# Attention scores of layer 1: the lo parts of q over all 128 rows beside zeros, the cached keys in a gap of the bias tile

## The chip, the cores and the metric

The kernel runs on one core of a Trainium2 chip. The metric is device time in microseconds (us), lower is better. A core has a tensor engine (PE; its weight loads are listed apart, as PEld), a vector engine (DVE), a scalar engine (ACT), GpSimd (POOL) and a sync engine (SP) whose queue issues nearly all DMAs here. Each engine works through its own list of instructions in order and waits for others by semaphores.

## What is computed

Two layers of a transformer trunk for 128 prompt tokens and 256 sample tokens, all in float32, D = 1024. Layer 0 has two recurrent mixers, layer 1 attention with 16 heads of 64 channels; an MLP ends each layer. Only layer 1's attention and the projection after it are touched by the change. In the reference, cut to that:

```python
qp, kp, vp = _na_qkv(hp, w_qkv_na[o], qn_na[o], kn_na[o])         # prompt: q and k with RMS norms per head
mp = _merge(_ctx_attention(qp, kp, vp)) @ w_out_na[o]              # softmax(q k / 8) v over the prompt's 128 keys
qs, ks_, vs = _na_qkv(hs, w_qkv_na[o], qn_na[o], kn_na[o])
ms = _merge(_na_latent(qs, ks_, vs, cache_na_k[:, o], cache_na_v[:, o], rpb_na[o])) @ w_out_na[o]
...
xp = xp + p_g1 * mp                                                # gates per condition: prompt, sample
xs = xs + s_g1 * ms
```

`_na_latent` puts a window of own keys (with a relative bias) and 128 cached keys into one softmax.

## The kernel before

**Products in parts.** Products of float32 accuracy are made of three products of rounded parts: hi times hi, lo times hi and hi times lo. ACT makes the hi part of a weight block (L211), DVE the lo part (L212). The main products have 128 rows of weights and 128 columns.

**Layer 1.** `layer1` runs over four groups b of 4 heads. For each it makes q, k (`attn_qk`) and v (`attn_v`) with the products of `tm_half` (L689 to L691, 256 columns each), loads the bias of the 4 heads (`na_bias`: 12 DMAs from DRAM into a tile of tag `bz`, L1532), and between these parts takes steps of the attention of the group before (`attn_heads`, `attn_pair`). After the loop come the steps of the last group, beside the first products of the output projection (`proj_residual`; its products are L674 to L676).

**q and k of a pair of heads** are transposed on PE (L1592; the cached keys L1604) to features by tokens, two heads in the 128 rows. For q the hi part is scaled out of PSUM by ACT (L1598), the lo part by one DVE instruction over 128 x 384 (L1599) into the tile `ql`. DMAs (L1588) copy the parts: `qd[:, e]` holds head e's hi part twice, in either half of the rows; `ks[:, e]` holds head e's hi part of k in its own half of the rows and the lo part in the other half.

**The scores of a head** are three pieces (prompt, two halves of the sample) of 256, 384 and 384 columns. Each is two products into the same PSUM piece: L1642 takes `qd` over 128 rows (hi of q with both parts of k), L1643 takes `ql` and `ks` over the 64 rows of the head alone (lo of q with hi of k). So a head has six products, by turns with 128 and 64 rows. DVE adds the bias and takes the maximum (L1649), ACT the exponentials (L1654), DVE the division (L1657), PE the transposes (L1662, L1666), ACT and DVE their copies (L1663, L1667), PE the products with v, by turns in the two column halves of the array (L1677, form 128*64).

```python
nc.tensor.matmul(p, qd[:, e, kt % 2, tt], ks[:, e, kt % 2, c], start=True, stop=False)
nc.tensor.matmul(p, ql[r, kt % 2, tt], ks[r, e, kt % 2, c], start=False, stop=True)
```

**Memory.** Tiles are taken from slots by tag, in turn (`sb`): a tile waits until the one that had its slot is done with. In layer 1's pool the tag `m4` has two slots. `attn_tiles` puts all cached keys (`kc`, one DMA, L1567) and all cached values (`vc`, L1569) in them; in the rows of the trace both are named `m`. After the attention `spread_gate` (called by `proj_residual`) takes two more tiles of this tag, the gates of prompt and sample spread over the partitions: `m<-gs`, L515, 512 KB each.

**After the attention** `residual` multiplies the projection's sums by the gate (L1273, per token tile and column half: prompt tile 0 reads the first gate tile, sample tiles 1 and 2 the second) and adds them to x (L1275, the first column half on POOL), and `norm` runs by token tile: squares on ACT (L544), L546, POOL's power (L528), the scaling of one half on DVE (L549) and the other on ACT (L550), transposes on PE (L555), then shift, scale and parts (L560 to L567). The MLP's first products (L1340 to L1342) need the tiles 0 and 1.

**Order.** The order of each engine is set by a scheduler at build time, from the order of the code, the slots and its own estimate of durations; `behind` pins a few places.

Of the kernel before, what the change touches and what calls it, by code (L numbers as in the profile page):

```python
# [30 lines left out]
# the levels inside blocks of 32  # L31
NS = 5
# the MLP's first blocks take the last token tile later, so that they need not wait for its norm
BEHIND = 2
# order of issue: what is put behind which marked instructions (see Trunk.behind) on their engines.
# "split", "group": weights and products (by column tile) of the first parts (PARTS); "gate1", "gate2": products of the output
# gates, by half of the rows; "proj", column half, token tile, half of the rows; "last": the last products of the MLPs,
# by layer, token tile and column half; T: a norm's transposes, by token tile and half; D, A: its last steps on VectorE
# and ScalarE (rD, rA: of the first norm); sel: of the modulation; s, out: of DeltaNet's states and outputs
# [11 lines left out]
# the first norm's features (row tiles) in parts, of which the modulation and the first products are taken one by one  # L51
PARTS = [range(0, 2), range(2, 4), range(4, 6), range(6, 8)]
# order of the mixers' part: h, d: steps of HGRN2 and DeltaNet (n of them), a: of the modulation; 256 columns of products:
# f: forget gates (2 direction + half), q: HGRN2's q, c: q, k, v of DeltaNet (of 6), v: values, g: output gates;
# m: output of HGRN2
# [4 lines left out]
# steps of the modulation beside the blocks of the two MLPs  # L60
PUMP = [0, 0, 4, 4] + [3, 4] * 6, [0] * 6 + [1] * 9 + [0]
# block of an MLP at which its gate is read
GATE_AT = 15
# halves of blocks of weights (of w1 by number, of the mixers' as in STEPS) whose lo part GpSimd takes, and the level at
# which it takes the products of HGRN2's gates
# [4 lines left out]
# names of the 128 x 128 constant matrices, in their order in the constants' array  # L70
# [3 lines left out]
def make_consts():  # L74
    """Constants that depend on shapes alone: matrices [128, n, 128] (row index a, column index b); per level L the
    pairs of positions in different halves of one block of 2L (levels up to 16 only inside the 32 x 32 blocks on the
    diagonal, [128, 32], behind the identity), side by side; and [128, 64] the column windows."""
# [11 lines left out]
    # column windows of the neighbourhood attention; queries (rows, twice 64) in reversed column order  # L89
# [7 lines left out]
class Halves:  # L97
    """[128, 8, n] as two tiles [128, 4, n], indexed as one."""
# [9 lines left out]
class Trunk:  # L108
# [15 lines left out]
    def open(self, name, **bufs):  # L124
        """A pool for a part of the program; bufs: slots by tag. Pools close in the reverse order."""
        st = self.ctx.enter_context(ExitStack())
        self.pools.append((st, bufs, st.enter_context(self.tc.tile_pool(name=name, bufs=1))))
# [4 lines left out]
    def banks(self, **tags):  # L132
        """PSUM's banks by tag, taken in turn, for a part of the program."""
        self.bank = {tag: list(b) for tag, b in tags.items()}
# [8 lines left out]
    def behind(self, *key):  # L143
        """What is traced here is issued behind the instructions that ORDER names, on their engines."""
# [34 lines left out]
    def split_tiles(self, tag):  # L179
        """Tiles of the hi and lo parts of [128, 8, 384]."""  # L180
        tiles = [self.sb([P, 4, T], tag, F32R) for _ in range(4)]
        return Halves(tiles[0::2]), Halves(tiles[1::2])
# [4 lines left out]
    def mixc(self, shape, name, dt=F32):  # L187
        """A tile that lasts as long as layer 0's mixers."""
# [12 lines left out]
    def slab(self, src, a, b, ring=""):  # L201
        """[128, a, b] of a weight matrix, in two halves along a."""
# [11 lines left out]
    def split_w(self, raws, a, b, ring="", pool=()):  # L214
        """hi and lo parts of a slab: functions of the index along a. pool: the halves whose lo part GpSimd takes."""
# [11 lines left out]
    def start(self):  # L227
# [47 lines left out]
        # silu(cond) by row tile, [128, 2 kt + cond]; a column tile takes 32 columns, of which the first two count  # L275
        self.sc = self.const([P, 2 * KT + 30], "scz")
        nc.gpsimd.memset(self.sc, 0.0)
        # column (kind, cond): 1 in rows 64 g + 32 kind + cond
# [6 lines left out]
    def params_ada(self):  # L285
        """The modulation's bias and the norms' gains, feature-major."""
# [5 lines left out]
    def params(self):  # L292
# [6 lines left out]
        # lower bound of the forget gate: softmax over the 3 rows, the first row of its running sum  # L299
# [16 lines left out]
    def ada_quad(self, l, cols, take):  # L316
        """Four blocks of 512 columns (from cols) of silu(cond) @ ada_w, one per column tile of the array:
        take(rows, psum [128, 512]), of block j the two conditions in rows 32 j and 32 j + 1. In steps."""
# [15 lines left out]
    def ada_sums(self, l, col, take):  # L334
        """1024 columns (from col) of silu(cond) @ ada_w, with the products on the other engines, beside the MLP's on
        the tensor engine, which takes only the sums over the partitions: take(psum [128, 512]), of half n of the
        columns condition v in row 64 v + 32 n. In steps."""
# [18 lines left out]
    def ada_half(self, l, col, take):  # L356
        """1024 columns (from col) of silu(cond) @ ada_w: column tile 2 g + n of the array takes half g of the rows and
# [1415 lines left out]
```

## Time and profile before

| | |
|---|---|
| time, median of 3 runs | 1180.23 us (1179.6 to 1186.71) |
| span of the profiled execution | 1183.9 us |
| its own time | not listed apart; of the three runs only the one of 1186.71 us is longer than this span |
| PE busy | 1127.1 us, 95% |
| DVE, ACT, POOL busy | 65%, 42%, 24% |
| share of the chain that ended last | PE 79%, POOL 6%, DVE 6%, DMA 6% |
| layer 1's attention | about 726 to 883 us of the span |

A matmul's record has a start and a modelled end; ends overlap the next starts. The pace is read from start to start. "128*128" is the part of the array that a product uses (rows by columns); 64*128 is half of its rows. Idle time is listed with what released it.

### The profile page before, as it was taken

The page shows a single profiled execution, that of the slowest core. Times are in us where ns is not written, and L with a number is a line of the kernel's source. Part 1 is how long each engine was busy: PE and PEld are TensorE (multiplying, and loading weights), DVE is VectorE, ACT ScalarE, POOL GpSimd, SP SyncE. Part 2 cuts the span into 40 slices and gives each one's busy share as a digit, 9 for nine tenths or more (in the row PEclk, how much of TensorE's full clock was granted, in tenths as well). Part 3 has the DMA queues.
Part 4 walks back from the last instruction along what each step waited for, and adds up shares of the span by engine and source line. Part 5 has one row for each costly group of instructions (what it writes and reads, how often), then busy time and mean ns, then how long its engine had stood idle before and what let it go on. Part 6 is the DMA issues. An engine that isn't in the chain of part 4 may idle for free.

```text
span 1183.9 us, 18507 instructions
## 1 busy us (share of the span) xinstructions
PE 1127.1 (95%) x7141; PEld 963.7 (81%) x7141; DVE 765.0 (65%) x1183; ACT 495.3 (42%) x853; POOL 288.5 (24%) x309
## 2 busy tenths in 40 slices
PE   6989879998898899999999999999997999999998
PEld 3858758977775788898889898888776999999987
DVE  4587798885254798986898565666656793333433
ACT  4564323432361553433442455555534644333331
POOL 0154991331311201111111333423003021111102
PEclk9989979998998899999999999999998999999999
DMA  8854535340242298775775237844612874344311
GB/s 297 279 162 140 173 125 153 91 140 5 72 133 81 82 348 269 259 243 186 235 246 161 72 86 182 213 127 129 180 55 71 318 227 131 113 131 130 107 36 54
DMA packets 141723, 184.67 MB, mean 156 GB/s; under 512 B 36435, under 2 KB 113317, under 8 KB 141637
## 3 DMA queue, kind: packets, MB, share of 16 engines
q1 hardware_dynamic: 141317, 183.44, 50.0%
q8 instruction: 56, 0.92, 0.3%
q14 instruction: 30, 0.25, 0.1%
q10 hardware_dynamic: 320, 0.07, 0.0%
HBM read 171.53 MB, written 4.61 MB: 149 GB/s over the span
## 4 chain that ended last, share of the span: by engine, by line
PE 79%; POOL 6%; DVE 6%; DMA 6%; issue 2%; SPq 1%; ACT 1%; POOLq 0%; DVEq 0%; ACTq 0%
PE tmp L1341 7%; PE tmp L1342 7%; PE acc L1326 7%; PE tmp L1340 7%; PE acc L1327 7%; PE acc L1328 7%; PE acc L689 3%; PE acc L690 3%; PE acc L691 3%; POOL sm L1062 2%; POOL sm L1063 2%; PE acc L647 2%; DMA ada<-in_ada_w 2%; PE acc L648 2%; PE acc L649 2%
## 5 line engine op out<-in xcount | busy, mean ns | idle before, releaser
L212 DVE TENSOR_TENSOR wlo<-raw,whi 128x1024 fp32r<-128x1024 f32 x192 | 244.5, 1283 | 161.2 <-ACT whi L211 148.3
L211 ACT ACTIVATE whi<-raw 128x1024 fp32r<-128x1024 f32 x198 | 206.1, 1050 | 318.2 <-PE acc L1328 201.8
L1360 POOL TENSOR_TENSOR h<-h 128x384 f32<-128x384 f32 x56 | 67.9, 1212 | 422.7 <-ACT h L1357 422.7
L1327 PE MATMUL acc<-wlo,h 128*128 128x512 f32 x380 | 148.6, 391 | 0.0
L1326 PE MATMUL acc<-whi,h 128*128 128x512 f32 x380 | 146.1, 393 | 0.0
L349 DVE SCALAR_TENSOR_TENSOR adc<-adr,scz,adc 128x1024 f32<-128x1024 f32 x98 | 128.1, 1337 | 9.8 <-DMA adr<-in_ada_w 9.6
L1328 PE MATMUL acc<-whi,h 128*128 128x512 f32 x380 | 121.3, 391 | 0.0
L1326 PEld LDWEIGHTS acc<-whi,h 128*128 128x128 f32 x380 | 71.2, 188 | 19.7 <-ACT whi L211 5.0
L1341 PE MATMUL tmp<-hyB,whi 128*128 128x384 f32 (+1 forms) x256 | 85.0, 332 | 2.3 <-DVE hyB L567 2.3
L1340 PE MATMUL tmp<-hyB,whi 128*128 128x384 f32 (+1 forms) x256 | 84.3, 332 | 2.5 <-DVE hyB L566 2.5
L1340 PE MATMUL tmp<-hyA,whi 128*128 128x384 f32 (+1 forms) x256 | 83.7, 333 | 3.2 <-DVE hyA L566 3.2
L1341 PE MATMUL tmp<-hyA,whi 128*128 128x384 f32 (+1 forms) x256 | 84.8, 332 | 0.4 <-DVE hyA L567 0.4
L1342 PE MATMUL tmp<-hyA,wlo 128*128 128x384 f32 (+1 forms) x256 | 84.6, 332 | 0.0
L689 PE MATMUL acc<-whi,hyB 128*128 128x256 f32 x288 | 84.2, 293 | 0.0
L690 PE MATMUL acc<-whi,hyB 128*128 128x256 f32 x288 | 83.4, 290 | 0.7 <-DVE hyB L567 0.6
L691 PE MATMUL acc<-wlo,hyB 128*128 128x256 f32 x288 | 83.1, 289 | 0.1
L1342 PE MATMUL tmp<-hyB,wlo 128*128 128x384 f32 (+1 forms) x256 | 83.1, 332 | 0.0
L1327 PEld LDWEIGHTS acc<-wlo,h 128*128 128x128 f32 x380 | 71.4, 188 | 14.3 <-DVE wlo L212 0.5
L1328 PEld LDWEIGHTS acc<-whi,h 128*128 128x128 f32 x380 | 71.1, 188 | 13.7
L647 PE MATMUL acc<-hyA,whi 128*128 128x384 f32 x208 | 74.7, 359 | 0.0
L648 PE MATMUL acc<-hyA,whi 128*128 128x384 f32 x208 | 72.6, 349 | 0.0
L649 PE MATMUL acc<-hyA,wlo 128*128 128x384 f32 x208 | 72.1, 348 | 0.0
(457 smaller groups left out, 2413.9 us busy)
## 6 DMA issues: line engine op xcount, KB each, us to landing
raw<-in_w_mlp SPq DMA_DIRECT2D x128, 512.0 KB, 4.4
adr<-in_ada_w SPq DMA_DIRECT2D x80, 512.0 KB, 4.7
raw<-in_w_in_ab SPq DMA_DIRECT2D x34, 512.0 KB, 4.9
raw<-in_w_qkv_na SPq DMA_DIRECT2D x24, 512.0 KB, 5.3
ada<-in_ada_w SPq DMA_DIRECT2D x32, 256.0 KB, 5.4
raw<-in_w_out_ab SPq DMA_DIRECT2D x8, 512.0 KB, 5.2
m<-gs SPq DMA_DIRECT2D x8, 512.0 KB
ks<-qk SPq DMA_DIRECT2D x32, 128.0 KB, 4.0
```

The lines of the kernel that those rows point to most:

```text
L211: self.nc.scalar.activation(hi, x, AF.Copy)
L212: (eng or self.nc.vector).tensor_tensor(lo, x, hi.bitcast(F32), op=ALU.subtract)
L349: nc.vector.scalar_tensor_tensor(acc[v], raw, s[v], acc[v], op0=ALU.mult, op1=ALU.add)
L689: nc.tensor.matmul(pg[:, t - t0], hhi[:, k, c], whi(k), start=(k == 0), stop=False)
L690: nc.tensor.matmul(pg[:, t - t0], hlo[:, k, c], whi(k), start=False, stop=False)
L691: nc.tensor.matmul(pg[:, t - t0], hhi[:, k, c], wlo(k), start=False, stop=(k == KT - 1))
L1326: nc.tensor.matmul(pg, shi, w2hi(n)[:, o], start=start, stop=False)
L1327: nc.tensor.matmul(pg, shi, w2lo(n)[:, o], start=False, stop=False)
L1328: nc.tensor.matmul(pg, slo, w2hi(n)[:, o], start=False, stop=last)
L1340: nc.tensor.matmul(pg[n], w1hi(k)[:, c], hhi[:, k, tc_], start=(k == 0), stop=False)
L1341: nc.tensor.matmul(pg[n], w1hi(k)[:, c], hlo[:, k, tc_], start=False, stop=False)
L1342: nc.tensor.matmul(pg[n], w1lo(k)[:, c], hhi[:, k, tc_], start=False, stop=(k == KT - 1))
```

## The change

The lo parts of q get tiles of their own that last for the whole of layer 1: two tiles `qlow` [128, 2, 2, 384], one per parity of the group. Head e's lo part lies in its half of the rows, and zeros (four POOL memsets, once) in the other half. The second product of the scores then runs over all 128 rows of `ql` and `ks`; the zeros cancel k's lo part. The lo part is written by two DVE instructions of 64 rows instead of one of 128.

The two `ql` tiles take 6 KB more of a partition together. `m4` goes from 2 slots to 1 and `pT` from 8 to 7 blocks, and the cached keys move from `m4` into the bias tile: of its five blocks of 128 columns per head the second was never used, and two heads' blocks hold a group's four heads of keys, loaded by two DMAs per group (`na_tile`, before the group's q). The transposes and reads of `pT` are renumbered. The diff without lines that only drop comments:

```diff
-    def na_bias(self, hg):
...
-        nc = self.nc
+    def na_tile(self, hg):
+
         b = self.sb([P, 4, 5, P], "bz")
+        self.kc = b[:, 0:2, 1]
+        for k in range(2):
+            h = 4 * hg + 2 * k
+            self.nc.sync.dma_start(b[:, k, 1].rearrange("p (h d) -> p h d", h=2),
+                                   self.i["cache_na_k"][0, 0, h:h + 2].rearrange("h s d -> s h d"))
+        return b
+
+    def na_bias(self, hg, b):
...
         nc, i = self.nc, self.i
-        self.kc = self.m4([P, NH, HD])
-        nc.sync.dma_start(self.kc, i["cache_na_k"][0, 0].rearrange("h s d -> s h d"))
         self.vc = self.m4([P, NH, HD])
         nc.sync.dma_start(self.vc, i["cache_na_v"][0, 0].rearrange("h s d -> s h d"))
+
+        self.qlow = [self.sb([P, 2, 2, T], "ql", F32R) for _ in range(2)]
+        for low in self.qlow:
+            for e in range(2):
+                nc.gpsimd.memset(low[64 - 64 * e:P - 64 * e, e].bitcast(F32), 0.0)
...
-        low = self.sb([P, 2, T], "ql", F32R) if kind == 0 else None
+        low = self.qlow[b % 2]
...
-                nc.vector.scalar_tensor_tensor(six(low[:, k]), src, qn, six(hi[:, 0:T].bitcast(F32)), op0=ALU.mult, op1=ALU.subtract)
+                for e, r in enumerate(half):
+                    nc.vector.scalar_tensor_tensor(six(low[r, e, k]), self.flip64(pt[r, 0:T]), qn[r], six(hi[r, 0:T].bitcast(F32)),
+                                                   op0=ALU.mult, op1=ALU.subtract)
...
-                nc.tensor.transpose(pt[:, 384:512], self.kc[:, 4 * b + 2 * k:4 * b + 2 * k + 2].rearrange("p h d -> p (h d)"),
+                nc.tensor.transpose(pt[:, 384:512], self.kc[:, k],
                                     self.c["ident"])
...
-            r = slice(e * 64, e * 64 + 64)
             (qd, ql), ks = qkv[0], qkv[1]
...
-                nc.tensor.matmul(p, ql[r, kt % 2, tt], ks[r, e, kt % 2, c], start=False, stop=True)
+                nc.tensor.matmul(p, ql[:, e, kt % 2, tt], ks[:, e, kt % 2, c], start=False, stop=True)
...
-            pT = self.sb([P, 8, P], "pT")
+            pT = self.sb([P, 7, P], "pT")
...
-                nc.tensor.transpose(pt[:, j], s[:, j], self.c["ident"])
+                nc.tensor.transpose(pt[:, j], s[:, (1, 2, 3, 0)[j]], self.c["ident"])
...
-            nc.vector.tensor_copy(pT[:, 3::2], pt)
+            nc.vector.tensor_copy(pT[:, 1:6:2], pt)
...
-                                 probs[e][:, 2 * j:2 * j + 2 if j else 1].rearrange("p a b -> p (a b)"),
+                                 probs[e][:, 2 * j - 2 if j else 6:2 * j if j else 7].rearrange("p a b -> p (a b)"),
...
-        self.open("spc", cm=1, qd=2, ql=2, ks=2, qk=4, v3=2, m4=2, bz=2, s=3, pT=4, g2=2, o=4, ss=4, ss8=4, mx=6)
+        self.open("spc", cm=1, qd=2, ql=2, ks=2, qk=4, v3=2, m4=1, bz=2, s=3, pT=4, g2=2, o=4, ss=4, ss8=4, mx=6)
...
-            qkv = []
+            qkv, bias = [], self.na_tile(b)
...
-            heads = self.attn_heads(b, qkv, self.na_bias(b), yy)
+            heads = self.attn_heads(b, qkv, self.na_bias(b, bias), yy)
```

The scheduler has made a new order of layer 1 on every engine; up to the first weights of layer 1 all orders are the same. Two places of it are shown. The first is SP's queue at the end of the attention, before; `m` are the two gate tiles, `raw` the halves of weight blocks, and each row ends with the semaphores that the issue waits for:

```order
L515 DMA m_1449_8448<-gs_5404 128x1024 [waits PE_49]
L206 DMA raw_8486<-in_w_out_na 128x2x512 [waits DMAHW7_49,DVE_49]
L1588 DMA ks_7949<-qk_8078 64x512 [waits DMAHW0_49,Activation_49]
L1588 DMA ks_7949<-qk_8078 64x512 [waits DMAHW1_49]
L1588 DMA ks_7949<-qk_8080 64x512 [waits DMAHW2_49,DVE_49]
L1588 DMA ks_7949<-qk_8080 64x512 [waits DMAHW3_49]
L206 DMA raw_8488<-in_w_out_na 128x2x512 [waits DMAHW4_49]
L206 DMA raw_8783<-in_w_mlp 128x4x256 [waits DMAHW5_49,DVE_49]
L206 DMA raw_8785<-in_w_mlp 128x4x256 [waits DMAHW7_49,DMAHW6_49,DVE_49]
L206 DMA raw_8897<-in_w_mlp 128x4x256 [waits DMAHW4_49,DVE_49]
L515 DMA m_1450_8449<-gs_5404 128x1024 [waits DMAHW0_49,PE_49]
L206 DMA raw_8899<-in_w_mlp 128x4x256 [waits DMAHW5_49,DMAHW1_49,DVE_49]
```

The same place now:

```order
L206 DMA raw_8502<-in_w_out_na 128x2x512 [waits DMAHW5_49,DVE_49]
L206 DMA raw_8504<-in_w_out_na 128x2x512 [waits DMAHW6_49,DVE_49]
L1600 DMA ks_7966<-qk_8095 64x512 [waits DMAHW7_49,Activation_49]
L1600 DMA ks_7966<-qk_8095 64x512 [waits DMAHW0_49]
L206 DMA raw_8799<-in_w_mlp 128x4x256 [waits DMAHW4_49,DMAHW1_49,DVE_49]
L1600 DMA ks_7966<-qk_8097 64x512 [waits DMAHW2_49,DVE_49]
L1600 DMA ks_7966<-qk_8097 64x512 [waits DMAHW3_49]
L206 DMA raw_8801<-in_w_mlp 128x4x256 [waits DMAHW5_49,DVE_49]
L206 DMA raw_8913<-in_w_mlp 128x4x256 [waits DMAHW6_49,DVE_49]
L515 DMA m_1446_8464<-gs_5404 128x1024 [waits PE_49]
L515 DMA m_1447_8465<-gs_5404 128x1024 [waits DMAHW7_49,DMAHW6_49,DVE_49]
L206 DMA raw_8915<-in_w_mlp 128x4x256 [waits DMAHW1_49,DMAHW0_49,DVE_49]
```

The first gate's load has moved behind the MLP's first weights, next to the second, and the second one waits for DVE where it waited for PE. The other place is DVE after the attention, before; `g` is a product of sums `acc` and gate `m`, `o` a half of a normalised token tile, `ss` its sum of squares:

```order
L1273 TENSOR_TENSOR g_1479_8600<-acc_8496,m_1449_8448 128x512
L1273 TENSOR_TENSOR g_1480_8603<-acc_8498,m_1449_8448 128x512
L1275 TENSOR_TENSOR x<-x,g_1480_8603 128x512
L1273 TENSOR_TENSOR g_1489_8641<-acc_8497,m_1450_8449 128x512
L1273 TENSOR_TENSOR g_1490_8644<-acc_8499,m_1450_8449 128x512
L546 TENSOR_SCALAR ss_8607<-ss_8606 128x1
L1275 TENSOR_TENSOR x<-x,g_1490_8644 128x512
L546 TENSOR_SCALAR ss_8607<-ss_8606,ss_8607 128x1
L546 TENSOR_SCALAR ss_8648<-ss_8647 128x1
L549 TENSOR_SCALAR o_8608<-x,ss_8607 128x512
L546 TENSOR_SCALAR ss_8648<-ss_8647,ss_8648 128x1
L549 TENSOR_SCALAR o_8649<-x,ss_8648 128x512
```

And now:

```order
L1273 TENSOR_TENSOR g_1476_8616<-acc_8512,m_1446_8464 128x512
L1273 TENSOR_TENSOR g_1477_8619<-acc_8514,m_1446_8464 128x512
L1275 TENSOR_TENSOR x<-x,g_1477_8619 128x512
L546 TENSOR_SCALAR ss_8623<-ss_8622 128x1
L546 TENSOR_SCALAR ss_8623<-ss_8622,ss_8623 128x1
L1273 TENSOR_TENSOR g_1486_8657<-acc_8513,m_1447_8465 128x512
L1273 TENSOR_TENSOR g_1487_8660<-acc_8515,m_1447_8465 128x512
L549 TENSOR_SCALAR o_8624<-x,ss_8623 128x512
L1275 TENSOR_TENSOR x<-x,g_1487_8660 128x512
L546 TENSOR_SCALAR ss_8664<-ss_8663,ss_8664 128x1
```

The sums of squares of the prompt's tile have moved ahead of the sample's first products with the second gate, and its scaling (L549) stands behind them as before.

## Rows read from the trace of the kernel before

**Rows 1.** The page: the span, the busy time of the engines, and the chain that ended last by engine.

```profile
span 1183.9 us, 18507 instructions
PE 1127.1 (95%) x7141; PEld 963.7 (81%) x7141; DVE 765.0 (65%) x1183; ACT 495.3 (42%) x853; POOL 288.5 (24%) x309
PE 79%; POOL 6%; DVE 6%; DMA 6%; issue 2%; SPq 1%; ACT 1%; POOLq 0%; DVEq 0%; ACTq 0%
```

**Rows 2.** Busy time of each engine in three stretches: the attention, what follows it up to the MLP's first products, and a part of the latter; the last columns are the granted clock, the DMA engines' busy share and GB/s.

```profile
726.00:883.00 157.00, 156.60 (x1006) 124.53 (x1006) 100.16 (x275) 81.24 (x189) 36.28 (x41) 1.00 0.54 142
883.00:910.00 27.00, 19.18 (x85) 14.98 (x83) 21.87 (x33) 13.25 (x27) 11.06 (x7) 0.88 0.26 79
893.00:897.00 4.00, 4.00 (x12) 3.17 (x12) 2.71 (x7) 3.20 (x7) 0.00 (x0) 0.57 0.01 2
```

**Rows 3.** What PE's products waited for between 726 and 910 us, all of it: us in total, times, longest.

```profile
PE tmp L1340 <- DVE hyB L566: 2.5, 1, 2.5
PE tmp L555 <- DVE o L549: 2.4, 1, 2.4
PE tmp L1341 <- DVE hyB L567: 2.3, 1, 2.3
PE sc L1642 <- DMA ks<-qk: 0.6, 1, 0.6
PE acc L674 <- ACT hyA L1681: 0.6, 1, 0.6
```

**Rows 4.** PE's timeline around one head's scores: start, duration, product, part of the array, size.

```profile
781.05 0.28 PE L691 MATMUL acc<-wlo,hyB 128*128 128x256 f32 x1
781.17 0.28 PE L1642 MATMUL sc<-ks,qd 128*128 128x256 f32 x1
781.38 0.38 PE L1643 MATMUL sc<-ks,ql 64*128 64x256 f32 x1
781.69 0.44 PE L1642 MATMUL sc<-ks,qd 128*128 128x384 f32 x1
782.06 0.44 PE L1643 MATMUL sc<-ks,ql 64*128 64x384 f32 x1
782.43 0.44 PE L1642 MATMUL sc<-ks,qd 128*128 128x384 f32 x1
782.80 0.44 PE L1643 MATMUL sc<-ks,ql 64*128 64x384 f32 x1
783.17 0.39 PE L689 MATMUL acc<-whi,hyB 128*128 128x256 f32 x1
783.39 0.28 PE L690 MATMUL acc<-whi,hyB 128*128 128x256 f32 x1
```

**Rows 5.** Two of the weight loads (PEld) in the same stretch.

```profile
781.38 0.18 PEld L1643 LDWEIGHTS sc<-ks,ql 64*128 64x128 f32 x1
...
783.17 0.19 PEld L689 LDWEIGHTS acc<-whi,hyB 128*128 128x128 f32 x1 [0.19 <-issue]
```

**Rows 6.** Two products of 384 columns in the MLP of layer 0, all with 128 rows (timeline of PE).

```profile
561.14 0.33 PE L1341 MATMUL tmp<-hyA,whi 128*128 128x384 f32 x1
561.32 0.33 PE L1342 MATMUL tmp<-hyA,wlo 128*128 128x384 f32 x1
```

**Rows 7.** The instructions that touch `ql` (view by tile): ns min/median/max, first and last start.

```profile
L1643 PEld LDWEIGHTS sc<-ks,ql x48: 182/183/183, 726.7 to 868.8; 64*128 64x128 f32 x48
L1599 DVE SCALAR_TENSOR_TENSOR ql<-tq,prm,qk x8: 587/614/622, 710.7 to 830.3; 128x384 fp32r<-128x384 f32 x8
```

**Rows 8.** GpSimd and SP where layer 1's pool begins (timelines): the first memsets and power, and the loads of the cached keys and values.

```profile
693.22 0.31 POOL L1515 MEMSET g<- 120x256 f32 x1 [6.75 <-DVE hyB L567]
693.47 0.52 POOL L1533 MEMSET bz<- 128x512 f32 x1
695.79 1.65 POOL L528 TENSOR_TENSOR ss<-ss,eps 128x8 f32<-128x8 f32 x1 [1.80 <-DVE ss L1553]
693.16 0.37 SPq L1567 DMA_DIRECT2D m<-in_cache_na_k  x1
705.24 3.87 SPq L1532 DMA_DIRECT2D bz<-rpb  x6
```

**Rows 9.** The end of the attention: the issues of the two gate tiles (SP), one us behind the second (busy times, clock, DMA share and GB/s as in rows 2), DVE's products with the gates, and its scaling of the first sample tile.

```profile
845.92 0.34 SPq L515 DMA_DIRECT2D m<-gs  x1
883.30 0.34 SPq L515 DMA_DIRECT2D m<-gs  x1
887.00:888.00 1.00, 1.00 (x6) 0.82 (x5) 1.00 (x1) 0.35 (x1) 0.61 (x1) 1.00 0.00 0
885.54 1.29 DVE L1273 TENSOR_TENSOR g<-acc,m 128x512 f32<-128x512 f32 x2 [1.16 <-PE acc L676]
888.09 1.28 DVE L1273 TENSOR_TENSOR g<-acc,m 128x512 f32<-128x512 f32 x2
892.75 0.49 DVE L549 TENSOR_SCALAR o<-x,ss 128x512 f32<-128x512 f32 x1 [0.67 <-POOL ss L528]
```

**Rows 10.** The last head: PE's last scores, DVE's division of them (three instructions) and PE's first transposes of them (timelines).

```profile
868.84 0.44 PE L1643 MATMUL sc<-ks,ql 64*128 64x384 f32 x1
873.80 0.95 DVE L1657 TENSOR_SCALAR s<-s,mx 128x128 f32<-128x128 f32 x3
878.25 0.60 PE L1662 MATMUL tr<-ident,s 128*128 128x128 f32 x4
```

More of the change, by code (lines that the diff above doesn't have):

```diff
@@ L1519, in na_bias_rows @@
         self.rpb = scr
-    def na_bias(self, hg):
+    def na_tile(self, hg):
+        b = self.sb([P, 4, 5, P], "bz")
+        self.kc = b[:, 0:2, 1]
[5 more added lines that the diff above has]
+    def na_bias(self, hg, b):
         nc = self.nc
-        b = self.sb([P, 4, 5, P], "bz")
         scr = self.rpb
```

## The prediction

> **What bounds the kernel now.** I read the page first, for the engine that carries the end: the chain that ended last lies on PE for 79%, and PE is busy for 95% of the span [rows 1]. Then the stretch that the change touches, by busy time: from 726 to 883 us PE is busy for 156.60 of 157.00 us at the full granted clock (1.00, that is 2.4 GHz), DVE for 100.16, ACT for 81.24, DMA for 0.54 [rows 2]. Then what PE waits for there: 0.6 us for the copies of k before the first scores and 0.6 us for ACT behind the last head, nothing else [rows 3]. So in the attention the end is set by PE's own list, and what shortens that list by a microsecond is worth a microsecond until another engine is late. Only behind the attention PE waits for others: 2.5, 2.4 and 2.3 us for DVE, in the norm before the MLP [rows 2, 3].
>
> A busy PE is not PE at its pace, so the third view is its timeline around one head [rows 4]. Products of 128 rows follow each other at 0.12 us per 256 columns (781.05 to 781.17), and 0.18 us per 384 columns in the MLP [rows 6]. The scores don't: 384 columns take 0.37 us (782.06 to 782.43), 256 take 0.21 to 0.31. The loads of weights tell why [rows 5]: L1643's load begins at 781.38, with its own product, and not during the product before it; likewise the load of L689 behind the last score, at 783.17. A load takes 0.18 to 0.19 us. Where the form goes from 128 to 64 rows or back, the load is not hidden.
>
> **The change part by part.**
>
> *The second product over 128 rows.* One head from its first score to the second product behind it takes 783.39 - 781.17 = 2.22 us [rows 4]. In one form the seven products would take 3 x 0.12 + 4 x 0.18 = 1.08 us [rows 4, 6]. That is 1.14 us per head, 18.2 us for 16 heads. A second way: six switches per head, 96 in all, each with one exposed load of 0.187 us, are 18.0 us. The columns streamed stay the same; the rows do not enter the pace. Where a head's scores are followed by L1677 (128*64) a switch stays, a few of the 96. Bounds: 18.2 us; or 18.2 x 12 / 16 = 13.7 us if the last four heads, which have only the projection's products beside them, are held by their softmax. I take 18.2 here and put that loss below.
>
> The Trainium skill, TensorEngine Tiling (Array Packing), section Key Properties, states that a change of tiling mode drains the engine; by that rule a stream in one mode would not, and the trace agrees as far as [rows 4, 6] go. The Trainium skill, TensorE: Matmul & The Clock Gate, section The mechanism, speaks against this change: a load overlaps a running product only if their row groups differ. By it the new products of 128 rows would hide nothing and the first term would be 0 (rival D); 128*128 products at 0.12 us with loads of 0.19 us say otherwise, so the sum goes by the rows.
>
> *Two DVE instructions for one* (L1599). Eight become sixteen. No instruction of 64 rows of this kind is in the rows; if it costs what 128 rows cost, 8 x 0.614 = 4.9 us more [rows 7], if it costs half, nothing. DVE has 157 - 100 = 57 us free in the stretch [rows 2], and the copies of `qd` by DMA start from ACT's part and run beside it. I take 0 on the path, 4.9 us if the cover is gone.
>
> *Four memsets on POOL.* The nearest row is 128 x 512 in 0.52 us [rows 8]; 768 columns by that are 0.78 us, four 3.1 us; not below 0 and hardly over 4. They stand behind L1515, which starts at 693.22 because the pool opens then, and ahead of the first L528, which started at 695.79. So that power, and q's scaling behind it, comes about 2 us later, while PE has the products of k and v to do. 0 on the path, 2 us if not.
>
> *Cached keys in eight loads for one.* Seven more issues on SP; six `bz` loads took 3.87 us, so 0.65 us each at most [rows 8], 4.5 us of SP over the layer, 1.8 us of it at its start. From the third group on they also wait until the bias tile of two groups earlier is read, but so did the bias loads; the transposes that need them come a whole q block later. 0, at most 2 us. The renumbered transposes and the smaller `pT` change nothing: the same instructions and slots.
>
> *One slot of `m4`.* This is the cost that the code does not announce. Before, the first gate took the slot of the cached keys and was loaded at 845.92, the second that of the values, at 883.30, when the last product with v was done [rows 9]. Now the first gate has to wait for the values, and the second for the first: SP's order shows them side by side, the second waiting for DVE. Call the end of the products with v T (883.3 before). The second gate's load, alone on the DMA engines, had landed by 887.0: the next us moves nothing [rows 9], so 3.7 us from issue to landing. Then:
> - first gate lands at T + 3.7; DVE's products of the prompt's tile start there instead of 885.54 = T + 2.2, and end at T + 5.0;
> - second gate is issued at T + 5.0, lands at T + 8.7; the sample's products start there instead of 888.09 = T + 4.8: 3.9 us later;
> - DVE's scaling of the prompt's tile stands behind these in the new order, that of the sample's tile, at 892.75 = T + 9.5 before, comes at T + 13 or so.
>
> Behind that DVE, not PE, leads to the MLP's first products (PE waits 2.5 and 2.3 us for it [rows 3]). DVE is not quite full there, 21.87 of 27.00 us [rows 2], so a part of the 3.9 us is taken up, and the projection's last products fill some of it. Bounds: 1.5 us (only the first gate's lateness counts) and 5 us (all of it, and a stretch at the lower clock, 0.57 as at 893 to 897 [rows 2], gets longer: that one is mostly at 1.2 GHz, after PE's wait of 2.4 us). I take 3.5, nearest to the plain shift of 3.9. SP's later weights lose nothing: the next one waits for a slot anyway.
>
> *New waits in the attention.* With 18.2 us less, PE needs everything 12% sooner: 157 - 18.2 = 138.8 us, in which DVE has 100.16 + 4.9 = 105 us to do, 76%, ACT 59%. In the tail the last head's division ends at 873.80 + 0.95 = 874.75, its transposes start at 878.25 [rows 10], 3.5 us later, so there was room. Bounds 0 and 6 us; I take 1.
>
> **The sum:** -18.2 + 3.5 + 1 = -13.7 us. The profiled span would go from 1183.9 to 1170.2; that span alone is 0.3% above the median of the runs, so the difference is put to the median: 1180.2 - 13.7 = **1166.5 us**.
>
> **The rivals.**
>
> *B, the gates cost nothing:* the projection's last products cover the second load. For it: DVE's idle time there. Against it: three waits for DVE on PE already [rows 3]. 1180.2 - 18.2 + 1 = 1163, or 1162 without new waits.
>
> *C, the heads' own chain takes over:* scores, maximum, exponentials, division, transposes. From the last score's end (868.84 and a pace of 0.37, 869.2) to its division's end (873.80 + 0.95) are 5.5 us [rows 10]; it decides where PE has less than this to do between a head's scores and its transposes. Against it: 3.5 us of room at the last head. For it: everything between has been re-ordered, and DVE goes to 76%. If half of the first term is lost: 1180.2 - 9.1 + 3.5 = 1174.6.
>
> *D, the loads stay exposed* (the other side: slower). The switch of rows would not be the cause; it could be the two operands, written by different engines, or the form of the accumulation. It decides if the products of the scores still start 0.3 us and more apart. Against it: L689 to L691 also accumulate and change weights every time, at 0.12 us. Then the gates' 3.5 us and up to 5 us of DVE stay: 1184 to 1189.
>
> **How the numbers follow.** Forecast (saving kept, gates 1.5 to 5, new waits up to 3; 1163.5 to 1170): 0.58. B: 0.14. C (1170 to 1177): 0.21. D: 0.07. About 1% is what a measurement of this kernel can tell from no change: 11.8 us, so 1168.4 and 1192.0 are the borders. Faster: B and all but 0.07 of the forecast, 0.65. Same: that 0.07, C, and half of D, 0.31. Slower by over 1% needs D and more lateness on top: 0.04. The range leaves out D and the farther half of C, and goes a microsecond below B: 1161 to 1173.
>
> **What would show it.** In the profile after: L1656 in form 128*128, scores 0.12 and 0.18 us apart, a head in about 1.1 us; no "issue" idle before its loads; the stretch of the attention shorter by 15 to 18 us. The second `m<-gs` some 5 us behind the first, both behind the last product with v, and L1273 idle for a DMA; PE's wait before the MLP longer by 2 to 5 us. Wrong would be: products of the scores still 0.3 us apart (D); PE waiting in L1675 or L1690 for ACT or DVE, several us in all (C); both gates early (B). Layer 0 and the MLPs should not move.

## The result, and the profile after

The changed kernel took 1167.74 us (median; 1165.11 to 1169.55) against 1180.37 us: ratio 0.9878, 95% interval 0.9852 to 0.9905. Measured twice more, beside the experiments below, it came to 0.9919 (0.9899 to 0.9938) and 0.9912 (0.9892 to 0.9932). Weighted by their intervals the three give 0.991, 11 us less: about 1%, at the border of what was to count as faster. 1166.5 us was predicted, 1161 to 1173; 0.991 is 1169 to 1170 us on that scale.

**The page of the changed kernel**: span, engines, and the chain that ended last.

```profile
span 1163.3 us, 18529 instructions
PE 1101.2 (95%) x7141; PEld 953.1 (82%) x7141; DVE 767.2 (66%) x1191; ACT 494.5 (43%) x853; POOL 286.9 (25%) x313
PE 80%; POOL 6%; DVE 6%; DMA 4%; issue 2%; ACT 1%; SPq 1%; ACTq 0%; DVEq 0%; POOLq 0%
```

PE still carries the end, with the same 7141 products. Now a head's scores, on **PE's timeline** (answers to [rows 4]) and one of **its weight loads** (answers to [rows 5]):

```profile
760.52 0.28 PE L1655 MATMUL sc<-ks,qd 128*128 128x256 f32 x1
760.64 0.28 PE L1656 MATMUL sc<-ks,ql 128*128 128x256 f32 x1
760.76 0.34 PE L1655 MATMUL sc<-ks,qd 128*128 128x384 f32 x1
760.94 0.34 PE L1656 MATMUL sc<-ks,ql 128*128 128x384 f32 x1
761.12 0.33 PE L1655 MATMUL sc<-ks,qd 128*128 128x384 f32 x1
761.29 0.34 PE L1656 MATMUL sc<-ks,ql 128*128 128x384 f32 x1
761.46 0.28 PE L689 MATMUL acc<-whi,hyB 128*128 128x256 f32 x1
761.58 0.28 PE L690 MATMUL acc<-whi,hyB 128*128 128x256 f32 x1
```

```profile
760.52 0.19 PEld L1656 LDWEIGHTS sc<-ks,ql 128*128 128x128 f32 x1
```

All is 128*128, 0.12 us per 256 columns and 0.18 per 384, and the load of L1656 begins with the product before it (760.52), not with its own (760.64). The head takes 761.58 - 760.52 = 1.06 us where it took 2.22. Summed from start to next start over all 96 score products, they take 15.7 us and took 31.9.

**Busy times** of the attention and what follows (columns as in [rows 2]), then **all that PE's products waited for** from 690 to 890 us (answers to [rows 3]):

```profile
726.00:864.00 138.00, 136.77 (x984) 119.09 (x982) 99.16 (x277) 78.52 (x185) 33.48 (x40) 1.00 0.56 154
864.00:890.00 26.00, 18.98 (x84) 14.75 (x85) 17.97 (x33) 13.33 (x29) 8.72 (x7) 0.93 0.28 90
```

```profile
PE tmp L555 <- ACT o L550: 2.3, 1, 2.3
PE tmp L555 <- DVE o L549: 1.6, 1, 1.6
PE acc L689 <- ACT o L1557: 1.4, 1, 1.4
PE tmp L1340 <- DVE hyB L566: 1.2, 1, 1.2
PE tmp L555 <- DVE s L560: 1.1, 1, 1.1
PE tmp L1341 <- DVE hyB L567: 0.7, 1, 0.7
PE acc L674 <- ACT hyA L1694: 0.6, 1, 0.6
PE sc L1655 <- issue: 0.6, 2, 0.4
PE acc L691 <- DVE wlo L212: 0.5, 1, 0.5
```

Two things differ. Ahead of the first scores PE waits 1.4 and 0.5 us that it did not wait before. Behind the attention its idle time is in more and shorter pieces: 1.2 and 0.7 us ahead of the MLP's products where it was 2.5 and 2.3. **The gates**: SP's issues, and DVE's reads (answer to [rows 9]):

```profile
863.55 5.14 SPq L515 DMA_DIRECT2D m<-gs  x2
867.04 1.29 DVE L1273 TENSOR_TENSOR g<-acc,m 128x512 f32<-128x512 f32 x2 [2.40 <-DMA m<-gs]
872.03 1.29 DVE L1273 TENSOR_TENSOR g<-acc,m 128x512 f32<-128x512 f32 x2 [1.30 <-DMA m<-gs]
876.76 0.48 DVE L549 TENSOR_SCALAR o<-x,ss 128x512 f32<-128x512 f32 x1
```

With T = 863.55 the prompt's products start at T + 3.5, the sample's at T + 8.5, and the sample's scaling at T + 13.2. Before they stood at T + 2.2, T + 4.8 and T + 9.5.

**Where the time went, by landmarks.** A: from POOL's L1515, where layer 1's pool opens, to the last products with v. B: from there to the MLP's first product. C: from there to the end. Each is a difference of starts in one trace (of the products with v, the start of the last row that PE's timeline has of them); names of experiments are explained below.

| kernel | A, us | B, us | C, us | sum |
|---|---|---|---|---|
| before | 189.43 | 23.79 | 277.46 | 490.68 |
| changed | 174.53 | 25.24 | 275.20 | 474.97 |
| changed, second and third trace | 174.07, 175.16 | 26.06, 25.82 | 275.23, 275.23 | 475.36, 476.21 |
| rows64 | 192.08 | 25.74 | 275.20 | 493.02 |
| one_run | 181.51 | 22.74 | 276.76 | 481.01 |
| gates_qd | 174.92 | 22.57 | 276.51 | 474.00 |
| late_qd, lazy_qd | 175.00, 174.55 | 22.57, 22.72 | 278.00, 276.60 | 475.57, 473.87 |
| weights_first | 174.79 | 25.82 | 275.20 | 475.81 |

By this layer 1 is 14.5 to 15.7 us shorter: A gives 14.3 to 15.4, B takes 1.5 to 2.3, C gives 2.2 back. A itself has two parts: from L1515 to the first score the three traces are 2.2 to 2.7 us longer than before (33.2 us), and from the first score to the last products with v 16.8 to 17.6 us shorter (156.2 us).

### The profile page after: what moved, and what is told of

It reads as the page before. It is cut to its first block, busy times and chain, and to the rows that moved or that the text cites. A ratio compares the mean times of both kernels' runs of the same rounds, so it can differ in the third digit from the quotient of the medians.

```text
span 1163.3 us, 18529 instructions
## 1 busy us (share of the span) xinstructions
PE 1101.2 (95%) x7141; PEld 953.1 (82%) x7141; DVE 767.2 (66%) x1191; ACT 494.5 (43%) x853; POOL 286.9 (25%) x313
## 4 chain that ended last, share of the span: by engine, by line
PE 80%; POOL 6%; DVE 6%; DMA 4%; issue 2%; ACT 1%; SPq 1%; ACTq 0%; DVEq 0%; POOLq 0%
PE tmp L1341 7%; PE tmp L1342 7%; PE tmp L1340 7%; PE acc L1326 7%; PE acc L1327 7%; PE acc L1328 7%; PE acc L689 3%; PE acc L690 3%; PE acc L691 3%; POOL sm L1062 2%; POOL sm L1063 2%; PE acc L647 2%; PE acc L648 2%; PE acc L649 2%; PE acc L674 2%
## 5 line engine op out<-in xcount | busy, mean ns | idle before, releaser
L212 DVE TENSOR_TENSOR wlo<-raw,whi 128x1024 fp32r<-128x1024 f32 x192 | 240.7, 1264 | 165.4 <-ACT whi L211 153.6
L1360 POOL TENSOR_TENSOR h<-h 128x384 f32<-128x384 f32 x56 | 65.0, 1161 | 427.9 <-ACT h L1357 426.7
L349 DVE SCALAR_TENSOR_TENSOR adc<-adr,scz,adc 128x1024 f32<-128x1024 f32 x98 | 127.2, 1329 | 10.2 <-DMA adr<-in_ada_w 10.0
L1327 PEld LDWEIGHTS acc<-wlo,h 128*128 128x128 f32 x380 | 71.4, 188 | 13.9 <-DVE wlo L212 0.2
L1328 PEld LDWEIGHTS acc<-whi,h 128*128 128x128 f32 x380 | 71.0, 188 | 13.7
```

What stands on the lines that cost most here:

```text
L212: (eng or self.nc.vector).tensor_tensor(lo, x, hi.bitcast(F32), op=ALU.subtract)
L349: nc.vector.scalar_tensor_tensor(acc[v], raw, s[v], acc[v], op0=ALU.mult, op1=ALU.add)
L1327: nc.tensor.matmul(pg, shi, w2lo(n)[:, o], start=False, stop=False)
L1328: nc.tensor.matmul(pg, slo, w2hi(n)[:, o], start=False, stop=last)
```

## Experiments

Ratios are to the kernel before on the same chip, with 95% intervals.

**rows64.** Everything of the change, but 64 rows again:

```diff
-                nc.tensor.matmul(p, ql[:, e, kt % 2, tt], ks[:, e, kt % 2, c], start=False, stop=True)
+                nc.tensor.matmul(p, ql[r, e, kt % 2, tt], ks[r, e, kt % 2, c], start=False, stop=True)
```

> The changed kernel, but the second product takes only the 64 rows of its head out of the zero-filled tile (as before the change); zeros, eight key loads, the gap of the bias tile and the single m4 slot stay. Theory (the saving is the loads exposed at 96 changes of form, about 17.5 us by the stretch from the first score to the last product with v): 1167.7 + 17 = 1184 to 1186 us, a head in 2.2 us again, so that the rest of the change costs 4 to 6 us. Rival (part of the gain comes from the new order of work and the layout, not from the rows): 1176 to 1181 us. Rival (the rest of the change is free): 1180.4 us.

1188.47 us, ratio 1.0035 (1.002 to 1.005), which is 1184.5 us on the scale of the expectation. In the traces every engine does its work in the same order as in the changed kernel, so the rows are all that differs. The 128 rows are worth 1.0035 - 0.991 = 1.25%, about 15 us (13 to 17 by the intervals), in the time, and 17.6 us in A (192.08 - 174.53); the rest of the change alone costs about 4 us. The score products take 31.9 us again, as before the change, and the 16 heads, each from its first score to the second product behind the last, 38.5 us, where the changed kernel takes 20.3: 18.2 us. Of the 2.65 us by which A is longer than before, 1.7 us is one stretch at the last head: over 4 us the granted clock was 0.57 on the mean, that is mostly the lower of its two levels of 1.2 and 2.4 GHz (busy times, clock third from last); ahead of it PE had done the last two heads' twelve score products at 0.31 to 0.37 us each, with no listed wait:

```profile
865.80:869.80 4.00, 4.00 (x15) 3.31 (x15) 2.88 (x13) 3.02 (x6) 0.00 (x0) 0.57 0.00 0
```

4 x (1 - 0.57) = 1.7 us. The theory holds; the rival that gives a part of the gain to the new order falls with the equal orders, and the one by which the rest is free with the interval.

**one_run.** The kernel before, its 64-row products kept, but one behind the other:

```diff
-            for t, p, c in ((0, p0[:, 0:256], slice(0, 256)), (1, p0[:, 128:512], slice(128, 512)), (2, p1, slice(128, 512))):
...
+            for t, low in ((0, 0), (0, 1), (1, 1), (2, 1), (1, 0), (2, 0)):
+                tt, c = slice(t * P, (t + 1) * P), slice(128, 512) if t else slice(0, 256)
+                first = low == (t > 0)
...
+                        st.enter_context(self.tc.issue_after(prev.ins))
```

> The kernel before, 64-row products kept, but in each head the three of them one behind the other: whole, 64, 64, 64, whole, whole rows (sums started accordingly; the order of the six is fixed). By its list on TensorE the runs of 64-row products go from 48 to 24, the changes of form from 96 to 48. Theory (a load is exposed where the form changes): 48 x 0.187 = 9 us less, 1171 us, and inside a run of 64-row products 384 columns take 0.18 us. Rival (64 rows as such expose the load of each product, two in a row of one head as well; and the first whole one behind them): 48 + 24 = 72 exposed loads, 4.5 us less, 1176 us, and 0.37 us inside a run. Rival (the alternation of operands or accumulation exposes them): no change, 1180 us.

1175.13 us, ratio 0.9930 (0.9909 to 0.9950), 8.3 us less. PE's timeline and loads at a head with all three in a row:

```profile
764.54 0.28 PE L1650 MATMUL sc<-ks,qd 128*128 128x256 f32 x1
764.75 0.39 PE L1648 MATMUL sc<-ks,ql 64*128 64x256 f32 x1
764.98 0.34 PE L1648 MATMUL sc<-ks,ql 64*128 64x384 f32 x1
765.16 0.33 PE L1648 MATMUL sc<-ks,ql 64*128 64x384 f32 x1
765.42 0.62 PE L1650 MATMUL sc<-ks,qd 128*128 128x384 f32 x2
```

```profile
764.75 0.18 PEld L1648 LDWEIGHTS sc<-ks,ql 64*128 64x128 f32 x1
764.86 0.31 PEld L1648 LDWEIGHTS sc<-ks,ql 64*128 64x128 f32 x2
765.41 0.19 PEld L1650 LDWEIGHTS sc<-ks,qd 128*128 128x128 f32 x1 [0.24 <-issue]
```

Inside the run 384 columns take 765.16 - 764.98 = 0.18 us, and the loads of the second and third 64-row product begin, from 764.86 on, under a product of the same 64 rows. At the two changes of form the loads begin with their own product (764.75, 765.41), and the products on either side take 0.21 to 0.28 us instead of 0.12 or 0.18. From its first score to the second product behind (765.99) this head takes 1.45 us, where one form takes 1.06 and six changes 2.22: 0.19 to 0.20 us a change. So the pace of whole rows holds inside a run: 64 rows as such expose no load, the change of form does; and the alternation of operands exposes none in the changed kernel, where it stays (760.52 to 761.46). (In A this run also has 4 us at a granted clock of 0.59, from 858.54 to 862.54. A is 189.43 - 181.51 = 7.9 us shorter than before the change; without the 4 x (1 - 0.59) = 1.6 us it would be 9.5, with 9.0 expected. The score products alone take 24.0 us, 7.9 less than before.)

**gates_qd.** The change, with the two gates in the slots of `qd`:

```diff
         scr1, m2 = self.gate[1, 0], self.mod[1, 1]
+        self.tag_gate = "qd"                       # "m4" again ahead of the MLP
```

> The changed kernel, but the two tiles of the output gate of the attention lie in the slots of qd (free behind the scores) and no longer in the one m4 slot, so both can be loaded ahead of the last products with v. Prediction's term (3.5 us): 1164.2 us. As the two traces read now (MLP's first product 1.4 us later behind the last product with v than before the change): 1166.3 us. Rival (the gates cost nothing, other lateness leads there): 1167.7 us. In all cases the sample's scaled tile (second L549) should come 3 to 4 us earlier behind the last product with v.

1169.44 us, ratio 0.9876 (0.9853 to 0.9900), 1165.7 us on the scale of the expectation, with an interval that holds all three of its values. The second L549 starts 879.57 - 869.42 = 10.2 us behind the last product with v, as before the change (892.75 - 882.65 = 10.1), and not 876.76 - 862.86 = 13.9, and B falls to 22.57 us. But C grows by 1.3 us. The MLP's start on PE in this kernel, then the busy times of its first 12 us here, in the changed kernel, and before:

```profile
891.99 1.19 PE L1340 MATMUL tmp<-hyB,whi 128*128 128x256 f32 x4 [2.90 <-DVE hyB L566]
895.05 0.58 PE L1341 MATMUL tmp<-hyB,whi 128*128 128x256 f32 x1 [1.86 <-DVE hyB L567]
```

```profile
891.99:903.99 12.00, 10.13 (x68) 9.84 (x69) 6.13 (x9) 3.79 (x9) 2.90 (x2) 0.75 0.37 120
```

```profile
888.10:900.10 12.00, 11.28 (x92) 11.07 (x93) 8.85 (x16) 6.46 (x14) 3.85 (x5) 1.00 0.40 119
```

```profile
906.44:918.44 12.00, 9.66 (x63) 9.45 (x64) 5.63 (x8) 3.20 (x8) 2.90 (x2) 0.72 0.37 121
```

With early gates PE waits in fewer pieces, the last 2.90 us long for DVE, and the granted clock at the MLP's start is 0.75 over 12 us, as before the change (0.72). With late gates its waits there are short, and the clock is 1.00. But the lower clock has not gone from the trace: in the changed kernel a part of B runs at it, in the norm, and in gates_qd B has none of it up to 891 us (busy times of the two):

```profile
873.50:877.50 4.00, 3.10 (x10) 2.68 (x11) 2.88 (x7) 3.02 (x8) 1.12 (x2) 0.57 0.00 0
869.42:891.00 21.58, 16.72 (x82) 12.90 (x77) 17.24 (x27) 11.60 (x26) 8.11 (x6) 1.00 0.09 26
```

So B is 2.5 to 3.5 us longer with late gates (25.24, 26.06, 25.82 against 22.57, 22.57, 22.72), an unknown part of it by the clock, and C is 1.3 to 2.8 us shorter. B and C together are 300.4, 301.3 and 301.1 us with late gates against 299.1, 300.6 and 299.3: on the mean the late gates cost 1.3 us. What puts the lower clock into the one part or the other was not tried by itself; but C is 275.2 to 275.6 us in all nine traces with late gates, and 276.5 to 278.0 in the other five, the kernel before among them.

**changed_again, changed_third.** The changed kernel, beside the runs that follow.

> The changed kernel once more, as the measure for the runs beside it: 0.988 of the kernel before, that is 14 us less.

> The changed kernel a third time, as the measure for the two runs beside it and for the result as a whole: 0.988 to 0.992 of the kernel before.

0.9919 and 0.9912, as told above: the first measurement was the lowest of three.

**The start: bias_act, bias_lazy, weights_first, zeros2, zeros_late.** In the changed kernel the weights of the second q block are issued 15.9 us behind L1515 (704.20 - 688.33), behind twelve bias loads; before, 7.6 us behind it (700.84 - 693.22). SP's queue there:

```profile
690.13 2.10 SPq L1527 DMA_DIRECT2D bz<-in_cache_na_k  x4
692.85 1.09 SPq L1518 DMA_DIRECT2D rpb<-g  x1
695.55 3.98 SPq L1541 DMA_DIRECT2D bz<-rpb  x6
699.74 0.45 SPq L1570 DMA_DIRECT2D out_cache_na_k<-g  x1
700.23 3.87 SPq L1541 DMA_DIRECT2D bz<-rpb  x6
704.20 0.55 SPq L206 DMA_DIRECT2D raw<-in_w_qkv_na  x1
```

Three ways to get the weights ahead: ACT issues the first group's bias loads; these are traced with the group's first head; or they are tied behind the weights on SP.

```diff
-                nc.sync.dma_start(b[...], src)
+                (nc.scalar if hg == 0 else nc.sync).dma_start(b[...], src)      # bias_act
...
+        bias = self.na_bias(b, bias)      # bias_lazy: in attn_heads
...
+            if b == 0:                    # weights_first: ahead of na_bias(0)
+                ahead = self.slab(i["w_qkv_na"][0][:, 256:512].rearrange("(k p) n -> p k n", p=P), KT, 256)
```

> The changed kernel, but the bias loads of the first group of heads are issued by ACT and not by SP, where they stand ahead of the weights of the next block. Theory (TensorE's two waits ahead of the first scores, 1.4 and 0.5 us, come from weights that were issued 8 us later than before the change, behind bias loads in SP's queue): both waits go, 1.9 us less, 1165.8 us. Rival (they come from the four memsets of zeros on POOL, which hold up the first power and so ACT's and DVE's work): they stay, 1167.7 us. Rival (ACT, which evacuates PSUM, is held up by the six issues): slower, 1168 to 1171 us.

> The changed kernel, but a group's bias loads are traced with its first head and not ahead of the next block of q; they stay on SP, and the next weights are issued behind two of them and no longer behind twelve. Theory (these weights' lateness makes TensorE's waits ahead of the first scores, 0.5 and 1.4 us): both waits go, 1.9 us less than the changed kernel, and the first score comes 2 us earlier. Rival (they come from POOL's memsets, which hold up the first power): the waits stay and the time is that of the changed kernel. Rival (the first heads now wait for their bias): the gain of 1.9 us is lost in waits of DVE behind the first scores.

> The changed kernel, but the weights of the second block of q are issued on SP ahead of the twelve bias loads of the first group (as before the change), and these are tied behind them. Theory (TensorE's waits ahead of the first score, 1.4 to 1.9 us in three traces of the changed kernel, and with them the 2.6 us by which the part up to the last product with v is longer than the rows alone make it, come from these weights' lateness): the waits go, the part from the pool's opening to the last product with v falls from 174.5 (174.1 to 175.4) to 172 to 173 us. Rival (something else takes the time, as copies of k that now come later behind the same queue, which the run with the late bias loads showed): other waits of the same size, the part stays at 174 to 175.5 us.

bias_act 0.9930 (0.9910 to 0.9950), bias_lazy 0.9907 (0.9889 to 0.9924), weights_first 0.9902 (0.9883 to 0.9922). What PE waited for at the start of each, in this order:

```profile
PE tq L1604 <- DVE ql L1612: 4.1, 2, 2.0
PE acc L689 <- ACT o L1557: 1.9, 1, 1.9
```

```profile
PE sc L1655 <- DMA ks<-qk: 2.5, 1, 2.5
PE tq L1604 <- DVE qk L1625: 1.2, 1, 1.2
```

```profile
PE sc L1658 <- DMA ks<-qk: 1.7, 1, 1.7
PE tq L1607 <- DVE ql L1615: 1.5, 1, 1.5
```

In bias_lazy and weights_first the changed kernel's two waits are gone, so those came from the late weights; but a wait for the copies of k comes in their place, and one for DVE with it (in weights_first 15 us behind the first score). A is 179.6, 175.3 and 174.8 us against the changed kernel's 174.1 to 175.2: none is clear of it on the short side. So the theory that this order costs 2 us falls: with each of these orders something else was late. bias_act, 0.9930 or 1172 us, is slower than even its third rival said. On ACT the issues stand between its own work: DVE's L1612 waits 7.2 us for its L1610 in this stretch, 2.9 in the changed kernel; its trace also has the clock at 0.57 from 716.5 to 720.5.

For POOL's memsets (3.10 us for four, ahead of the first power, which starts 4.4 us behind L1515; before, 2.6) one run wrote the zeros twice, another put the memsets behind the first powers (`issue_after` the power; SP's and ACT's lists unchanged, PE's and DVE's but for a few neighbours):

> The changed kernel, but each half of the zeros is written twice: eight memsets on POOL instead of four, 3.1 us more ahead of the first power. Prediction (hidden, PE has products of k and v to do): no change. Rival (POOL's lateness reaches TensorE through the power, q's scaling and the evacuations): up to 3 us slower, with longer waits ahead of the first score.

> The changed kernel, but the four memsets of zeros stand in POOL's list behind the first powers (two behind the powers of the first q and k, two behind those of the second q) instead of ahead of all; every other list has its order. Theory, as the run with the zeros written twice now reads (in its trace 3 us more of memsets made layer 1's part up to the MLP 3 us longer, though its time did not show it): the memsets cost about as much as they take, so TensorE's waits ahead of the first score go from 1.4 to 1.9 us down to under 0.6 and the part from the pool's opening to the MLP gets 1.5 to 3 us shorter. Rival (prediction: hidden): the waits and the part stay within 0.5 us.

zeros2 0.9915 (0.9892 to 0.9938), zeros_late 0.9908 (0.9892 to 0.9924): both like the changed kernel beside them. In zeros_late the power starts 694.82 - 692.25 = 2.6 us behind L1515 again, and what PE waits for at the start is what it was (the second trace of the changed kernel has 0.7, 0.5 and 0.2):

```profile
PE acc L689 <- ACT o L1557: 0.9, 1, 0.9
PE acc L691 <- DVE wlo L212: 0.5, 1, 0.5
PE acc L689 <- ACT whi L211: 0.5, 1, 0.5
```

A is 176.3 us, not shorter. So the memsets are hidden, as predicted. zeros2 shifted the order of PE's and SP's lists too, and its trace has the clock at 0.57 from 728 to 732, 1.7 us by itself: its longer trace was no sign of a cost of the memsets.

**lazy_qd, late_qd.** gates_qd with bias_lazy, and gates_qd with zeros_late:

> The changed kernel with both: late bias loads and the gates in the slots of qd. If the two losses are as the traces read (1.9 us at the start; 1 to 2.7 us at the gates, a part of which the wait of the MLP's second product takes back): 3 to 4 us less than the changed kernel. If both are hidden: the same time.

> The changed kernel with both: the memsets of zeros behind the first powers and the gates in the slots of qd. If the losses are real and apart: 1.5 to 3 us for the zeros, 1 to 2 us for the gates (behind what the MLP's start takes back), so 2.5 to 5 us less than the changed kernel. If the zeros are hidden: 1 to 2 us less.

0.9889 (0.9869 to 0.9909) and 0.9892 (0.9876 to 0.9908). The three kernels with early gates are at 0.9876, 0.9889 and 0.9892, the changed kernel at 0.9878, 0.9919 and 0.9912: some 2 us better on the mean, at the border of what the intervals separate. Beside the changed kernel measured with them lazy_qd is 3.5 us less, as expected of both losses, and late_qd 2.4, nearer to the gates alone; the intervals overlap, and the traces show no gain at the start for either (A 174.6 and 175.0).

## Why the prediction was right

**The first term held.** 96 exposed loads, 18.2 us. A head with nothing between its scores went from 2.22 to 1.06 us where 1.08 was worked out, and all 16 together, rows64 against the changed kernel, give 38.5 - 20.3 = 18.2 us. The score products give 31.9 - 15.7 = 16.2 us of it, the products beside them the rest. On the way to the time some of it is lost: 16.8 to 17.6 us from the first score to the last products with v, about 15 us in the ratios. rows64 and one_run show the mechanism from two sides. Rival D falls. The rule that speaks for it (the Trainium skill, TensorE: Matmul & The Clock Gate, section The mechanism: loads overlap only where row groups differ) does not hold here: loads of the same 128 rows run under the product before (760.52), and so do those of the same 64 rows in one_run (764.86). The other one (the Trainium skill, TensorEngine Tiling (Array Packing), section Key Properties: a change of tiling mode drains the engine) fits: the time goes where the form changes. Its price in this case is that of one load, 0.19 to 0.20 us a change.

**The gates: the course was right, the size not.** "Lands at T + 3.7", "8.7", "T + 13 or so" were 3.5, 8.5 and 13.2. The term of 3.5 us is also about what the lateness costs at the MLP's first product, against kernels with early gates (2.5 to 3.5, a part of it by the clock). Two things in it failed. Against the kernel before B grows only by 1.5 to 2.3 us. Its gates were early (second L549 10.1 us behind the last products with v), but its trace has a stretch at the lower clock in B (0.57 from 893 to 897 [rows 2]), where the projection's products start 0.43 us apart instead of 0.23; the transposes behind them start 897.28 - 882.65 = 14.6 us behind the last products with v, in gates_qd 13.1. one_run, with the gates of the kernel before, has the clock at 1.00 there and B at 22.74. And the bounds said that a stretch at the lower clock "gets longer"; instead the one at the MLP's start went away, and C is 2.2 us shorter. So against the kernel before the term measures about 0 (B and C together -0.8 to 0.0 us), as in rival B, but not for its reason: the gates were late, and a stretch at the lower clock that the trace of the kernel before has is gone. That the whole came near the forecast is in part luck: against that trace 3.5 us were taken here that were not lost, and the way to the first score lost 2.2 to 2.7 us, for which the sum had 1 us at most.

**New waits: 1 us taken, about 2 measured**, and elsewhere than looked for. None in the heads (L1675 and L1690 wait for neither ACT nor DVE, rival C falls), but 1.4 to 1.9 us at the start, behind SP's list. There the key loads were costed at "0, at most 2 us", and what the scheduler put ahead of the next weights at nothing. With another order of that list other waits came, so what the start costs beyond these waits stays open.

**The parts costed at nothing.** L1612 takes 616 ns (median) for 64 rows, as long as 128 rows took [rows 7], so the upper bound, 4.9 us more of DVE, came true and in the changed kernel nobody waited for it. A memset was 0.73 us, a key load's issue 0.46 us (medians).

**The sum** of 13.7 us stands against 14.5 to 15.7 us by landmarks and 11 us by the three ratios. What lies between stays open. The kernel before has one trace, and its own time isn't known: every other trace here is of a run that took 1.7 to 1.9 us more than its span, which would make it some 1185.7 us, 5 us above the median of its runs (1179.6, 1180.2, 1180.5 and 1186.71 us).

## What to carry to other kernels

A product over part of the rows is not free of cost because it is smaller: look at the start-to-start pace, and where the form changes from one product to the next count one exposed load for each change. Fill the rows with zeros if there is memory for them, or put the products of one form side by side, which gave more than half of the gain with no memory at all. And price a wait together with the clock around it: here kernels with early gates ran the MLP's start at the lower clock and those with late gates a part of the norm, so that B and C together differ by 1.3 us where B alone differs by 2.5 to 3.5.

## What was not expected

The granted clock falls for 4 us, to 0.57 and 0.59, at the last heads of rows64 (no listed wait ahead) and one_run (0.74 us of wait ahead), and not at the last heads of the changed kernel. The exposed loads alone don't explain it: the kernel before has them all and a clock of 1.00 there [rows 2]. The cause is open. In layer 0, where all lists are the same, two executions of the changed kernel differ (busy times, first the one of 1163.3 us span, then the one of 1169.2 us):

```profile
200.00:300.00 100.00, 92.16 (x970) 81.39 (x957) 73.46 (x135) 34.08 (x59) 28.74 (x31) 1.00 0.30 93
```

```profile
200.00:300.00 100.00, 94.95 (x964) 83.79 (x949) 72.36 (x135) 33.57 (x58) 25.83 (x30) 0.95 0.29 89
```

From 300 to 406 us the clock is 0.94 and 0.90. Layer 1's pool opened at 688.3 us in the first, at 693.8 in the second. That is half of the gain that was to be measured, and why one measurement of few runs was not enough.
